# A gated-linear-attention layer on one core: TensorE's order of a head fixed from end to end, and the state updates of a PSUM bank issued together

## The chip, the cores and the metric

The kernel runs on one core of a Trainium2 chip. A core has TensorE (PE; its weight loads are listed apart as PEld), VectorE (DVE), ScalarE (ACT), GpSimd (POOL) and SyncE (SP), which issues most of the transfers. The metric is the device time of one execution in microseconds, lower is better. Before the change it is 3444.64 us, the median of three runs (3440.78 to 3449.58).

## The reference

Two layers work on 1024 latent tokens and 256 context tokens of width 1024, all in fp32. Layer 0 (neighbourhood attention and an mLSTM) is not touched. Layer 1 has 16 heads of HGRN2, a gated linear attention in both directions, which begins with a state that the context tokens leave. Cut to one head and one direction:

```python
q, f_fwd, f_bwd, i, z = split(h @ w_in)            # 128 columns each per head
f = lb + (1 - lb) * sigmoid(f_pre)                 # forget gate, per token and key column
k, lf, v = 1 - f, log(f), i
S = sum over context of (k * decay to the end) v^T # first state
# over chunks of the latent tokens, b = cumsum(lf) inside a chunk
o = (q * exp(b)) @ S + tril(q k^T with exp(b_t - b_s)) @ v
S = exp(b_last) * S + (k * exp(b_last - b))^T @ v
out = out + (rms(o_forward + o_backward) * h_norm * silu(z)) @ w_out
```

## The kernel before, in words

The loop over the 16 heads takes the span from about 2187 to 3337 us, and one head some 69 us. Products of projections are made of three TensorE products each (a high and a low part of either operand, L131 to L133).

A head h goes through these steps. `hg_f` makes its two forget gates F for 1280 tokens: 24 products 128x256 for the context and twice 24 products 128x512 for the latent tokens, each followed by a sigmoid on ACT (L983) and a scaling on DVE (L984); the forward gate comes from DRAM. `hg_vt` makes the context values (24 products, two transposes). `hg_intra` makes K = 1 - F (L1228), the sums ks (L1235) and Q (L1237) on DVE, and on PE the diagonal blocks as 16 strips of 64x64 (L1261, masked at L1248). Seven calls of `hg_level` then double the reach: each copies keys on ACT (gksel, L1297), makes 16 strips on PE (L1261) and updates Q and K on DVE (L1292). `hg_vz` makes values and the gate z of the latent tokens in eight runs of 24 products 128x256, read by ACT (L1188, L1190) and DVE (L1191). `hg_ctx` makes the two first states from the context (ACT gknc L1212, PE L1217). `hg_close` transposes the decayed keys of 8 chunks of 128 tokens (16 transposes, L1273) and ACT copies them (gkn, L1275).

`hg_scan` makes the states and the output. A backward update is a PE product (L1337) and a DVE step (L1339), seven in a chain; then each of 8 chunks has three products into the one accumulator bank `acc` (A times v L1349, Q times the backward state L1350, Q times the forward state L1351), and a forward update (L1354, DVE L1356). After 4 chunks ACT squares the bank (L1365), and DVE makes y4, the bank times z, into tile gA (L1369), which frees the bank for the other 4 chunks; POOL scales y4. `hg_out` transposes the result (L1408), ACT writes gyt (L1411), and POOL sends it to DRAM. Then POOL handles sums of output weights (`wo_sums`) and, for some heads, differences of earlier outputs (`y_diff`): two loads, a subtraction, three writes of 256 KB.

PSUM has 8 banks in the loop: two for products (mm), two for transposes (tr), three for strips and states (s), one for the accumulator (acc).

The order on each engine is set by a list scheduler, which runs a model of the engines while the program is built; code order gives the priority, `urgent()` raises it, and `issue_after(ins)` lets an instruction come only after another. Before, the eight runs of `hg_vz` are tied to the levels' strips, the gates of the next head to the last level, and everything else goes where the scheduler sees room.

Of the kernel before, what the change touches and what calls it, by code (L numbers as in the profile page):

```python
# [19 lines left out]
P = 128  # L20
# [25 lines left out]
class Prog:  # L46
# [99 lines left out]
    def proj_tr(self, ps, w, c0, t0, n):  # L146
        hh, hl = self.hh, self.hl
        s, c = slice(t0, t0 + n), slice(c0, c0 + P)
        self.dense(
# [820 lines left out]
    def hg_f(self, h, pool, w=None, run=None):  # L970
# [7 lines left out]
        for t0, n in ((LAT, CTX), (512, 512), (0, 512)):  # L978
            ps = self.ps("mm", [P, n])
            with self.tc.issue_after(run.ins) if run else ExitStack():  # L980
                self.proj_tr(ps, w, 0, t0, n)
# [3 lines left out]
        return F, Fc  # L985

    def hg_proj(self, h, pool, FF=None, run=None):
        dma = self.nc.sync.dma_start
        F, Fc = FF or self.hg_f(h, pool, run=run)
# [6 lines left out]
        return dict(F=F, Fc=Fc, q=q)  # L996
# [164 lines left out]
    def hg_vt(self, h, st, pool, w=None):  # L1161
# [5 lines left out]
        self.proj_tr(ps, w, 0, LAT, CTX)  # L1167
# [9 lines left out]
    def hg_vz(self, st, pool, runs):  # L1177
        nc, v, w = self.nc, st["v"], st["wz"]
        st["ss"] = [self.t(pool, [P, 4], F32, "gss", 2) for _ in range(2)]
        z = self.t(pool, [P, NT - 2, P], F32, "gz", 1)  # L1180
        runs = iter(runs)
        for tt in (6, 4, 2, 0):

            ps = self.ps("mm", [P, 2, 256])
            for j in range(2):
                with self.tc.issue_after(next(runs).ins):
                    self.proj_nat(ps[:, j, :], w, tt + j, 0, 256)
            nc.scalar.copy(v[:, tt : tt + 2, :], ps[:, :, 0:P])  # L1188
            sg = self.t(pool, [P, 2, P], F32, "gsg", 1)
            nc.scalar.activation(sg, ps[:, :, P:256], AF.Sigmoid)  # L1190
            nc.vector.tensor_tensor(out=z[:, tt : tt + 2, :], in0=sg, in1=ps[:, :, P:256], op=ALU.mult)  # L1191
        st["z"] = z


    def hg_ctx(self, st, pool):
# [17 lines left out]
        S = []  # L1213
        for d in range(2):
            u = self.ps("s", [P, P])
            for j in range(2):
                nc.tensor.matmul(u, lhsT=kn[:, 2 * d + j, :], rhs=v[:, 8 + j, :], start=(j == 0), stop=(j == 1))  # L1217
            s = self.t(pool, [P, P], F32, f"gS{d}", 10 if d else 2)
            nc.vector.tensor_copy(s, u)
# [4 lines left out]
    def hg_intra(self, h, st, pool):  # L1224
# [8 lines left out]
        for hf in (1, 0):  # L1233
            s = slice(hf * 512, (hf + 1) * 512)
            nc.vector.tensor_tensor(out=ks[hf], in0=K[:, 0, s], in1=K[:, 1, s], op=ALU.add)  # L1235
            for d in range(2):
                nc.vector.tensor_tensor(out=Q[:, 1 - d, s], in0=q[hf], in1=F[:, d, s], op=ALU.mult)  # L1237
        hv = dict(Q=Q, K=K, T=F, D=self.t(pool, [P, 8, 64], F32, "gD", 1))
        hv["A"] = self.t(pool, [P, 8, P], F32, "gA", 1)
# [814 lines left out]
```

## Time and profile before

| | before |
|---|---|
| median of three runs | 3444.64 us (3440.78 to 3449.58) |
| profiled execution | 3439.37 us, span 3437.3 us |
| mean granted TensorE clock | 0.994 of full speed |
| busy, share of the span | PE 97%, PEld 86%, DVE 63%, ACT 42%, POOL 24% |

The span is the part of the execution that the trace covers, and the difference of 2 us lies around it. A busy share is the time in which an engine has at least one instruction running; PE's matmuls are pipelined, so that two rows can overlap. Times in the rows of a timeline are us from the span's start, then the duration, then what the engine waited for just before, if it did.

### The profile page before, as it was taken

How to read it: one execution, taken by the hardware profiler on the slowest of the kernel's cores; microseconds unless marked ns; L12 is line 12 of the kernel's file. 1: busy time of each engine (PE TensorE's matmuls, PEld its weight loads, DVE VectorE, ACT ScalarE, POOL GpSimd, SP SyncE). 2: the span in 40 equal slices, each digit the busy share in tenths (PEclk: the TensorE clock that was granted, in tenths of full speed). 3: DMA queues.
4: the chain of work that ended last, by engine and by line, in shares of the span. 5: the costliest groups of instructions: out<-in, count | busy, mean ns of one | idle time of the engine just before them, and what ended most of it. 6: DMA issues, size and time to landing. Idle time of an engine off the chain costs nothing.

```text
span 3437.3 us, 64829 instructions
## 1 busy us (share of the span) xinstructions
PE 3329.7 (97%) x24814; PEld 2940.7 (86%) x24814; DVE 2179.7 (63%) x4965; ACT 1451.0 (42%) x3389; POOL 838.5 (24%) x1215
## 2 busy tenths in 40 slices
PE   7999999999999999999998999999999999999999
PEld 6699899998899888898877888888888888888887
DVE  5346666666645576686677555666666676667657
ACT  5335554445533444454453333333333333333343
POOL 2222222222221121221025333122232233234110
PEclk9999999999999999999999999999999999999999
DMA  7612322223234343354642333322232233224267
GB/s 250 229 53 78 92 82 73 79 67 92 82 100 138 106 143 110 121 171 142 221 132 77 105 102 101 104 70 76 87 97 88 76 96 83 76 76 101 54 187 205
DMA packets 338101, 379.80 MB, mean 110 GB/s; under 512 B 34600, under 2 KB 269800, under 8 KB 336768
## 3 DMA queue, kind: packets, MB, share of 16 engines
q1 hardware_dynamic: 286032, 236.73, 23.4%
q0 software_dynamic: 51760, 138.94, 12.9%
q8 instruction: 195, 3.19, 0.4%
q14 instruction: 114, 0.93, 0.1%
HBM read 272.31 MB, written 103.08 MB: 109 GB/s over the span
## 4 chain that ended last, share of the span: by engine, by line
PE 85%; DVE 4%; issue 4%; DMA 3%; ACT 2%; POOL 1%; SPq 1%; DVEq 0%; POOLq 0%; ACTq 0%
PE mm L131 16%; PE mm L132 15%; PE mm L133 15%; PE s L1261 4%; PE mm L923 3%; PE mm L924 3%; PE mm L925 3%; PE acc L861 2%; PE tr L841 2%; PE acc L633 2%; PE s L642 2%; PE x L133 1%; PE x L131 1%; PE x L132 1%; PE acc L1350 1%
## 5 line engine op out<-in xcount | busy, mean ns | idle before, releaser
L131 PE MATMUL mm<-wh,hh 128*128 128x256 f32 (+1 forms) x1504 | 466.2, 310 | 2.2 <-DVE graw L1550 0.8
L132 PE MATMUL mm<-wl,hh 128*128 128x256 f32 (+1 forms) x1504 | 464.1, 309 | 0.0
L133 PE MATMUL mm<-wh,hl 128*128 128x256 f32 (+1 forms) x1504 | 461.6, 307 | 0.0
L131 PE MATMUL mm<-hh,wh 128*128 128x512 f32 (+1 forms) x1160 | 421.7, 364 | 4.7 <-DVE og L959 3.1
L132 PE MATMUL mm<-hl,wh 128*128 128x512 f32 (+1 forms) x1160 | 422.9, 365 | 0.0
L133 PE MATMUL mm<-hh,wl 128*128 128x512 f32 (+1 forms) x1160 | 422.3, 364 | 0.4 <-DVE wl L74 0.4
L131 PEld LDWEIGHTS mm<-wh,hh 128*128 128x128 f32 x1504 | 284.8, 189 | 21.4 <-ACT ev L352 3.4
L132 PEld LDWEIGHTS mm<-wl,hh 128*128 128x128 f32 x1504 | 284.9, 189 | 12.3 <-issue 0.7
L133 PEld LDWEIGHTS mm<-wh,hl 128*128 128x128 f32 x1504 | 284.7, 189 | 12.0 <-issue 0.5
L131 PE MATMUL mm<-wzh,hh 128*128 128x256 f32 x960 | 284.8, 297 | 0.0
L133 PE MATMUL mm<-wzh,hl 128*128 128x256 f32 x960 | 272.6, 284 | 0.0
L132 PE MATMUL mm<-wzl,hh 128*128 128x256 f32 x960 | 272.4, 284 | 0.0
L131 PEld LDWEIGHTS mm<-hh,wh 128*128 128x128 f32 x1160 | 219.3, 189 | 41.7 <-ACT ev L371 4.2
L133 PEld LDWEIGHTS mm<-hh,wl 128*128 128x128 f32 x1160 | 219.2, 189 | 33.1 <-DVE wl L74 1.0
L132 PEld LDWEIGHTS mm<-hl,wh 128*128 128x128 f32 x1160 | 219.5, 189 | 29.7 <-issue 0.2
L131 PEld LDWEIGHTS mm<-wzh,hh 128*128 128x128 f32 x960 | 183.3, 191 | 7.2
L1297 ACT COPY gksel<-gK 128x1024 f32<-128x1024 f32 x96 | 110.5, 1151 | 178.6 <-DVE gK L1292 77.3
L132 PEld LDWEIGHTS mm<-wzl,hh 128*128 128x128 f32 x960 | 184.2, 192 | 0.0
L133 PEld LDWEIGHTS mm<-wzh,hl 128*128 128x128 f32 x960 | 183.5, 191 | 0.0
L74 DVE TENSOR_TENSOR wl<-wraw,wh 128x512 fp32r<-128x512 f32 x176 | 120.1, 690 | 74.9 <-ACT wh L73 71.7
L1292 DVE TENSOR_TENSOR gQ<-gQ,gF 128x1024 f32<-128x1024 f32 x112 | 142.3, 1271 | 34.6 <-PE s L1261 34.5
L1292 DVE TENSOR_TENSOR gK<-gK,gF 128x1024 f32<-128x1024 f32 x112 | 152.3, 1360 | 6.7
(562 smaller groups left out, 8512.3 us busy)
## 6 DMA issues: line engine op xcount, KB each, us to landing
wraw<-in_wab_dram SPq DMA_DIRECT2D x108, 256.0 KB
wraw<-yd SPq DMA_DIRECT2D x92, 256.0 KB
br<-in_wc_dram SPq DMA_DIRECT2D x64, 256.0 KB
md<-ev POOLq DMA_DIRECT2D x60, 256.0 KB, 2.6
wraw<-in_wc_dram SPq DMA_DIRECT2D x120, 128.0 KB
mloz<-md SPq DMA_DIRECT2D x40, 256.0 KB
s<-gyt POOLq DMA_DIRECT2D x36, 256.0 KB, 5.3
adar<-in_wada_dram SPq DMA_DIRECT2D x16, 512.0 KB
```

Source lines behind the costliest of these rows:

```text
L74: nc.vector.tensor_tensor(out=lo, in0=x, in1=hi.bitcast(F32), op=ALU.subtract)
L131: mm(ps, lhsT=lh(k), rhs=rh(k), start=(start and k == 0), stop=False, skip_group_check=skip)
L132: mm(ps, lhsT=lh(k), rhs=rl(k), start=False, stop=False, skip_group_check=skip)
L133: m = mm(ps, lhsT=ll(k), rhs=rh(k), start=False, stop=(stop and k == nk - 1), skip_group_check=skip)
L633: nc.tensor.matmul(num, lhsT=qc[:, j, :], rhs=C[d][:, j, :], start=False, stop=(j == 1))
L642: nc.tensor.matmul(u, lhsT=st["k"][c][:, j * P : (j + 1) * P], rhs=vw, start=True, stop=True)
L923: mm(ps, lhsT=yh[k], rhs=w.h(kk), start=(kk == 0), stop=False)
L924: mm(ps, lhsT=yh[k], rhs=w.l(kk), start=False, stop=False)
L925: mm(ps, lhsT=yl[k], rhs=w.h(kk), start=False, stop=(kk == 8 * len(qs) - 1))
L1261: return self.nc.tensor.matmul(out[s], lhsT=lhsT, rhs=rhs, start=True, stop=True, tile_position=(0, b * 64))
L1292: nc.vector.tensor_tensor(out=v, in0=v, in1=tot, op=ALU.mult)
L1297: m = nc.scalar.copy(ksel.rearrange("p (b s i) -> p b s i", s=2, i=h), pick(K))
```

## The change

The order of a head on PE is now written out. `last_pe` holds PE's last instruction of the piece before, and `seg()` lets a piece be issued only after it. The whole row of a head is: the diagonal strips; the strips of level 0 directly behind them; transposes of the context values; run 0 of `hg_vz`; level 1; first half of the previous head's `hg_out`; run 1; level 2; its second half; run 2; `hg_ctx`; then a level and a run in turn to level 6 and runs 6 and 7; `hg_close` for chunks 4 to 7; the next head's gate products for the context; `hg_close` for chunks 0 to 3; the backward updates of chunks 4 to 7, then 1 to 3, and the forward ones of chunks 0 to 3; 24 gate products 128x512; the forward updates of chunks 4 to 6; 24 gate products 128x512; the scan of chunks 0 to 3 and of chunks 4 to 7; and the next head's 24 products for the context values.

All updates of a bank are issued together (`hg_states`), and DVE's chain of steps reads them afterwards (`hg_chain`). So all states of both directions are kept: gS0 and gS1 have 8 buffers each (2 and 10 before). Besides, the sigmoid is written into z itself, the tile gA is taken only at level 6, `hg_out`, `wo_sums` and `y_diff` of a head come at levels 1 and 2 of the next, K's sums and Q are urgent, and `hg_ctx` uses one bank for both directions. 

```diff
+    @contextmanager
+    def seg(self):
+        with self.tc.issue_after(self.last_pe.ins) if self.last_pe else ExitStack():
+            yield
...
+        def part(t0, n):
             ps = self.ps("mm", [P, n])
-            with self.tc.issue_after(run.ins) if run else ExitStack():
-                self.proj_tr(ps, w, 0, t0, n)
+            with self.seg():
+                m = self.proj_tr(ps, w, 0, t0, n)
+            if self.pinned:
+                self.last_pe = m
...
+        parts = [lambda x=x: part(*x) for x in ((LAT, CTX), (512, 512), (0, 512))]
+        return F, Fc, parts
...
-                with self.tc.issue_after(next(runs).ins):
-                    self.proj_nat(ps[:, j, :], w, tt + j, 0, 256)
+                with self.seg():
+                    self.last_pe = self.proj_nat(ps[:, j, :], w, tt + j, 0, 256)
+                if j == 0:
+                    yield
+            z2 = z[:, tt : tt + 2, :]
             nc.scalar.copy(v[:, tt : tt + 2, :], ps[:, :, 0:P])
-            sg = self.t(pool, [P, 2, P], F32, "gsg", 1)
-            nc.scalar.activation(sg, ps[:, :, P:256], AF.Sigmoid)
-            nc.vector.tensor_tensor(out=z[:, tt : tt + 2, :], in0=sg, in1=ps[:, :, P:256], op=ALU.mult)
-        st["z"] = z
...
+        u = self.ps("s", [P, 2, P])
         for d in range(2):
-            u = self.ps("s", [P, P])
             for j in range(2):
-                nc.tensor.matmul(u, lhsT=kn[:, 2 * d + j, :], rhs=v[:, 8 + j, :], start=(j == 0), stop=(j == 1))
-            s = self.t(pool, [P, P], F32, f"gS{d}", 10 if d else 2)
-            nc.vector.tensor_copy(s, u)
+                nc.tensor.matmul(u[:, d, :], lhsT=kn[:, 2 * d + j, :], rhs=v[:, 8 + j, :], start=(j == 0), stop=(j == 1))
+        for d in range(2):
+            s = self.t(pool, [P, P], F32, f"gS{d}", 8)
+            nc.vector.tensor_copy(s, u[:, d, :])
...
+        halves = [(hf, slice(hf * 512, (hf + 1) * 512)) for hf in (1, 0)]
+        with self.urgent():
+            for hf, s in halves:
+                nc.vector.tensor_tensor(out=ks[hf], in0=K[:, 0, s], in1=K[:, 1, s], op=ALU.add)
+            for hf, s in halves:
+                for d in range(2):
+                    nc.vector.tensor_tensor(out=Q[:, 1 - d, s], in0=q[hf], in1=F[:, d, s], op=ALU.mult)
...
-        with self.urgent():
+        with self.urgent(), self.seg():
...
-        runs = [m]
+        self.last_pe = m
+        tiles = self.hg_vz(st, pool)
         for lev in range(7):
-            runs.append(self.hg_level(hv, lev, pool))
+            if lev == 6:
+                hv["A"] = self.t(pool, [P, 8, P], F32, "gA", 1)
+            self.hg_level(hv, lev, pool)
+            if lev in (1, 2) and prev:
+                prev(lev)
+            next(tiles)
             if lev == 2:
                 S = self.hg_ctx(st, pool)
-        return hv, S, runs
+                if prev:
+                    prev(3)
+        next(tiles)
+        return hv, S
...
+    def hg_states(self, st, H, d, c0, c1):
+        v = st["v"]
+        u = self.ps("s", [P, 4, P])
+        with self.seg():
+            for c in range(c0, c1):
+                m = self.nc.tensor.matmul(
+                    u[:, c - c0, :], lhsT=H["kn"][c // 4][d][:, c % 4, :], rhs=v[:, c, :], start=True, stop=True
+                )
+        self.last_pe = m
+        return {c: u[:, c - c0, :] for c in range(c0, c1)}
+
+
+    def hg_chain(self, H, d, S, u, order, pool):
+        for c in order:
+            s = self.t(pool, [P, P], F32, f"gS{d}", 8)
+            self.nc.vector.scalar_tensor_tensor(
+                out=s, in0=S[c], scalar=H["T"][:, d, c : c + 1], in1=u[c], op0=ALU.mult, op1=ALU.add
+            )
+            S[c + 1 if d == 0 else c - 1] = s
...
-        sb = {7: Sb}
-        for c in range(7, 0, -1):
-            if c in (7, 3):
-                u4 = self.ps("s", [P, 4, P])
-            u = u4[:, c % 4, :]
-            nc.tensor.matmul(u, lhsT=H["kn"][c // 4][1][:, c % 4, :], rhs=v[:, c, :], start=True, stop=True)
-            s = self.t(pool, [P, P], F32, "gS1", 10)
-            nc.vector.scalar_tensor_tensor(
-                out=s, in0=sb[c], scalar=H["T"][:, 1, c : c + 1], in1=u, op0=ALU.mult, op1=ALU.add
-            )
-            sb[c - 1] = s
         for c in range(8):
             cs = slice(c * P, (c + 1) * P)
             if c % 4 == 0:
                 o4 = self.ps("acc", [P, 4, P])
-                u4 = self.ps("s", [P, 4, P])
             o = o4[:, c % 4, :]
-            nc.tensor.matmul(o, lhsT=H["A"][:, c, :], rhs=v[:, c, :], start=True, stop=False)
-            nc.tensor.matmul(o, lhsT=H["Q"][:, 0, cs], rhs=sb[c], start=False, stop=False)
-            nc.tensor.matmul(o, lhsT=H["Q"][:, 1, cs], rhs=Sf, start=False, stop=True)
-            if c < 7:
-                u = u4[:, c % 4, :]
-                nc.tensor.matmul(u, lhsT=H["kn"][c // 4][0][:, c % 4, :], rhs=v[:, c, :], start=True, stop=True)
-                s = self.t(pool, [P, P], F32, "gS0", 2)
-                nc.vector.scalar_tensor_tensor(
-                    out=s, in0=Sf, scalar=H["T"][:, 0, c : c + 1], in1=u, op0=ALU.mult, op1=ALU.add
-                )
-                Sf = s
...
                 for h in range(16):
-                    self.hg_vt(h, st, pool, None if h else wv)
-                    hv, S, runs = self.hg_intra(h, st, pool)
-                    self.hg_vz(st, pool, runs)
-                    self.hg_close(hv, pool)
-                    self.hg_scan(st, hv, S, pool)
-                    if h < 15:
-                        st = self.hg_proj(h + 1, pool, run=runs[7])
+                    hv, (Sf, Sb) = self.hg_intra(h, st, pool, prev)
+                    nxt, parts = self.hg_proj(h + 1, pool) if h < 15 else (None, [lambda: None] * 3)
+                    self.hg_close(hv, 1, pool)
+                    parts[0]()
+                    self.hg_close(hv, 0, pool)
+                    Sf, Sb = {0: Sf}, {7: Sb}
+                    ub = self.hg_states(st, hv, 1, 4, 8)
+                    ub.update(self.hg_states(st, hv, 1, 1, 4))
+                    uf = self.hg_states(st, hv, 0, 0, 4)
+                    self.hg_chain(hv, 1, Sb, ub, range(7, 0, -1), pool)
+                    self.hg_chain(hv, 0, Sf, uf, range(4), pool)
+                    parts[1]()
+                    uf = self.hg_states(st, hv, 0, 4, 7)
+                    self.hg_chain(hv, 0, Sf, uf, range(4, 7), pool)
+                    parts[2]()
+                    self.hg_scan(st, hv, Sf, Sb, pool)
+                    st = nxt
                     if h == 15:
                         rh.close()
                         yp = es.enter_context(tc.tile_pool(name="oy", bufs=1, side="right"))
                         last = [self.t(yp, [P, 512], F32R, t, 1) for t in ("lasth", "lastl")] + [yp]
-                    y15 = self.hg_out(h, hv["A"], pool, self.yd2, last)
-                    if h < 14:
-                        self.wo_sums(h // 2, h % 2, pool, ("gknc", 1), ("gEc", 1))
-                    if h in (11, 12):
-                        self.wo_sums(7, h - 11, pool, ("gyt", 1), ("wraw", 3))
-                    if 0 < h < 9:
-                        self.y_diff(h - 1, pool)
+
+                    def prev(lev, h=h, A=hv["A"]):
+                        if lev == 3:
+                            return sums(h)
+                        self.hg_out(h, A, pool, self.yd2, None, (0,) if lev == 1 else (4,))
+
+                    def sums(h):
+                        if h < 14:
+                            self.wo_sums(h // 2, h % 2, pool, ("gknc", 1), ("gEc", 1))
+                        if h in (11, 12):
+                            self.wo_sums(7, h - 11, pool, ("gyt", 1), ("wraw", 3))
+                        if 0 < h < 9:
+                            self.y_diff(h - 1, pool)
+
+                    if h == 15:
+                        y15 = self.hg_out(h, hv["A"], pool, self.yd2, last)
+                    if h < 15:
+                        self.hg_vt(h + 1, st, pool)
```

Three places show how the order moved. The line numbers of the changed kernel are larger by 9 to 24 in these functions. **PE around the two halves of the scan**, a head of the middle; before (acc_27565 is the first half's bank, acc_27600 the second half's):

```order
L131 MATMUL mm_28047<-wzh_27773,hh_20307 128x256
L1351 MATMUL acc_27565<-gS_5478_27577,gQ_24854 128x128 [waits DVE_49]
L1354 MATMUL s_27566<-gv_27049,gkn_27533 128x128
L1349 MATMUL acc_27565<-gv_27049,gA_27092 128x128
L1350 MATMUL acc_27565<-gS_5470_27553,gQ_24854 128x128
...
L133 MATMUL mm_28047<-wzh_27773,hl_20308 128x256
L1351 MATMUL acc_27565<-gS_5479_27583,gQ_24854 128x128 [waits DVE_49]
L1354 MATMUL s_27566<-gv_27049,gkn_27533 128x128
L1354 MATMUL s_27601<-gv_27049,gkn_27519 128x128 [waits DVE_49]
L1349 MATMUL acc_27600<-gv_27049,gA_27092 128x128 [waits DVE_49]
L1350 MATMUL acc_27600<-gS_5469_27550,gQ_24854 128x128
```

and with the change (acc_27669 and acc_27691):

```order
L1383 MATMUL acc_27669<-gS_5468_27599,gQ_24854 128x128
L1381 MATMUL acc_27669<-gv_26995,gA_27416 128x128
L1382 MATMUL acc_27669<-gS_5463_27589,gQ_24854 128x128
L1383 MATMUL acc_27669<-gS_5469_27601,gQ_24854 128x128
L1381 MATMUL acc_27691<-gv_26995,gA_27416 128x128 [waits DVE_49]
L1382 MATMUL acc_27691<-gS_5462_27587,gQ_24854 128x128
...
L1382 MATMUL acc_27691<-gS_5422_27244,gQ_24854 128x128
L1383 MATMUL acc_27691<-gS_5475_27640,gQ_24854 128x128
L131 MATMUL mm_27736<-hh_20307,wzh_27714 128x256
L132 MATMUL mm_27736<-hl_20308,wzh_27714 128x256
L133 MATMUL mm_27736<-hh_20307,wzl_27713 128x256
L131 MATMUL mm_27736<-hh_20307,wzh_27714 128x256
```

Before, gate, value and z products stood between the scan's products; now both halves stand in one row, and the products of the next head (the last four rows) come behind them.

**DVE at the same place.** Before, and then with the change:

```order
L1356 SCALAR_TENSOR_TENSOR gS_5478_27577<-gS_5477_27571,gT_27293,s_27566 128x128 [waits PE_49]
L1248 TENSOR_TENSOR gD_27836<-s_27838,glm_4216_20266 128x512 [waits PE_49]
L1356 SCALAR_TENSOR_TENSOR gS_5479_27583<-gS_5478_27577,gT_27293,s_27566 128x128 [waits DVE_49,PE_49]
L1237 TENSOR_TENSOR gQ_24854<-gq_27731,gF_27632 128x512 [waits DMAHW4_49,PE_49]
L1237 TENSOR_TENSOR gQ_24854<-gq_27731,gF_27632 128x512 [waits PE_49]
L1356 SCALAR_TENSOR_TENSOR gS_5480_27589<-gS_5479_27583,gT_27293,s_27566 128x128 [waits DVE_49,PE_49]
L1205 TENSOR_SCALAR gq_27926<-gFc_27633 128x512 [waits DVE_49]
L1356 SCALAR_TENSOR_TENSOR gS_5484_27606<-gS_5480_27589,gT_27293,s_27601 128x128 [waits DVE_49]
L1369 TENSOR_TENSOR gA_27092<-acc_27565,gz_27301 128x512 [waits Activation_49,Pool_49]
```

```order
L993 TENSOR_SCALAR gF_27494<-gF_27494,lb_114 128x512 [waits Activation_49]
L1242 TENSOR_SCALAR gK_27767<-gF_27494 128x2048 [waits DVE_49]
L1253 TENSOR_TENSOR gQ_24854<-gq_27512,gF_27494 128x512 [waits DMAHW4_49,PE_49]
L1250 TENSOR_TENSOR gkn_27770<-gK_27767 128x512 [waits DVE_49]
L1250 TENSOR_TENSOR gkn_27769<-gK_27767 128x512
L1253 TENSOR_TENSOR gQ_24854<-gq_27512,gF_27494 128x512 [waits PE_49]
L1315 TENSOR_TENSOR gK_27767<-gK_27767,gF_27494 128x2x512 [waits DVE_49,Activation_49]
L1393 TENSOR_TENSOR gA_27416<-acc_27669,gz_27081 128x512 [waits Activation_49,Pool_49]
L1253 TENSOR_TENSOR gQ_24854<-gq_27510,gF_27494 128x512 [waits DMAHW2_49,PE_49]
L1253 TENSOR_TENSOR gQ_24854<-gq_27510,gF_27494 128x512 [waits PE_49]
L1393 TENSOR_TENSOR gA_27416<-acc_27691,gz_27081 128x512 [waits Activation_49]
```

y4 (L1369, now L1393, from the first bank) stood among the forward steps (L1356, now L1366) and the next head's diagonal; now it stands behind the next head's whole gate, K, ks, Q of one half and the first update of K, and the steps are done earlier.

**ACT and PE at the close of a head.** ACT before, and then with the change (wzh and wh are casts of the next weights, gkn the copies of transposed keys):

```order
L1275 COPY gkn_26029<-tr_26024 128x512 [waits PE_49]
L1275 COPY gkn_26036<-tr_26031 128x512 [waits PE_49]
L983 ACTIVATE gFc_26143<-mm_26156 128x256 [waits PE_49]
L73 CAST wzh_26283<-wraw_26299 128x512 [waits DMAHW3_49,DMAHW2_49]
L73 CAST wh_26890<-wraw_26891 128x512 [waits DMAHW4_49]
L73 CAST wh_26896<-wraw_26897 128x512 [waits DMAHW5_49]
L1275 COPY gkn_26043<-tr_26038 128x512 [waits PE_49]
L1275 COPY gkn_26050<-tr_26045 128x512 [waits PE_49]
L983 ACTIVATE gF_26142<-mm_26183 128x512 [waits PE_49]
```

```order
L1298 COPY gkn_26039<-tr_26034 128x512 [waits PE_49]
L1298 COPY gkn_26046<-tr_26041 128x512 [waits PE_49]
L992 ACTIVATE gFc_26015<-mm_26048 128x256 [waits PE_49]
L1298 COPY gkn_26080<-tr_26075 128x512 [waits PE_49]
L73 CAST wzh_26234<-wraw_26250 128x512 [waits DMAHW3_49,DMAHW2_49]
L1298 COPY gkn_26087<-tr_26082 128x512 [waits PE_49]
L73 CAST wh_26757<-wraw_26758 128x512 [waits DMAHW4_49]
L73 CAST wh_26763<-wraw_26764 128x512 [waits DMAHW5_49]
L992 ACTIVATE gF_26014<-mm_26125 128x512 [waits PE_49]
```

PE with the change (tr are the transposes, s the banks of the updates):

```order
L1296 MATMUL tr_26075<-ident_82,gK_25555 128x128 x3
L1296 MATMUL tr_26082<-ident_82,gK_25555 128x128 [waits Activation_49]
L1296 MATMUL tr_26082<-ident_82,gK_25555 128x128 x3
L1356 MATMUL s_26089<-gv_25523,gkn_26046 128x128 x4
L1356 MATMUL s_26094<-gv_25523,gkn_26087 128x128 [waits Activation_49]
L1356 MATMUL s_26094<-gv_25523,gkn_26087 128x128 x2
L1356 MATMUL s_26098<-gv_25523,gkn_26080 128x128 x4
L131 MATMUL mm_26125<-hh_20307,wh_26017 128x512 [waits DVE_49]
```

The last gkn copy now stands behind the fourth wzh cast as both copies of its half did before, but the two copies are split around it, and PE's second group of updates reads it directly, ahead of the gate products.

91 lines of the change are left out of this document (49 added, 42 removed).

## The prediction, made before the changed kernel was run

> **What bounds the kernel now.** I read the page first, then the busy time by head, then what TensorE's two queues waited for in the layer-1 loop, then single rows of the timeline. The page's first part and two rows and the sum of the windows by head (us, then busy us and instructions of PE, PEld, DVE, ACT, POOL, the granted clock, DMA share, GB/s):
>
> ```profile
> PE 3329.7 (97%) x24814; PEld 2940.7 (86%) x24814; DVE 2179.7 (63%) x4965; ACT 1451.0 (42%) x3389; POOL 838.5 (24%) x1215
> ...
> 2573.40:2641.80 68.40, 64.87 (x660) 59.81 (x659) 45.90 (x73) 24.11 (x54) 19.96 (x29) 1.00 0.28 88
> 2779.30:2849.70 70.40, 66.44 (x661) 61.29 (x660) 45.79 (x73) 23.94 (x53) 21.15 (x27) 0.98 0.35 90
> ...
> sum 1041.20, PE 983.53 PEld 906.41 DVE 684.44 ACT 360.63 POOL 288.97; mean PE 65.57 PEld 60.43 DVE 45.63 ACT 24.04 POOL 19.26
> ```
>
> TensorE bounds everything; DVE is at 66% in the loop. One head takes 1041.20 / 15 = 69.4 us, of which PE is idle 3.8. So the change, which leaves the instructions as they are, can win a few us per head, and can lose as many as it puts in TensorE's way. Its waits in the loop, from the queue that loads weights:
>
> ```profile
> PEld s L1354 <- DVE gS L1356: 23.0, 15, 1.6
> PEld s L1337 <- DVE gS L1339: 18.5, 31, 0.6
> PEld acc L1350 <- DVE gS L1339: 9.5, 15, 0.6
> PEld s L1354 <- DVE gS L1339: 8.8, 14, 0.6
> PEld s L1217 <- ACT gknc L1212: 8.4, 15, 0.6
> PEld acc L1349 <- DVE gA L1369: 8.0, 15, 0.9
> PEld s L1261 <- DVE gQ L1237: 4.7, 15, 0.3
> ```
>
> The first four are the state updates, where PE and DVE take turns in one PSUM bank. The timeline shows one turn:
>
> ```profile
> 2593.09 0.49 PE L1337 MATMUL s<-gv,gkn 128*128 128x128 f32 x2 [0.37 <-DVE gS L1339]
> 2594.02 0.49 PE L1337 MATMUL s<-gv,gkn 128*128 128x128 f32 x2 [0.44 <-DVE gS L1339]
> ...
> 2595.27 0.39 PE L1351 MATMUL acc<-gS,gQ 128*128 128x128 f32 x2
> ...
> 2596.39 0.39 PE L1350 MATMUL acc<-gS,gQ 128*128 128x128 f32 x2
> ```
>
> A turn costs 2594.02 - 2593.09 = 0.93 us, while five steps of products that wait for nothing take 1.12, or 0.224 each: 0.7 us lost per turn.
>
> **What it removes.** All updates of a bank are issued before DVE reads it, so the first four waits go: 23.0 + 18.5 + 9.5 + 8.8 = 59.8 us. DVE's fourteen chain steps remain, but under F's products. The wait for gA (8.0) changes its form and is priced anew below; gQ's 4.7 goes too, since 24 products stand ahead of the diagonal strips and cover DVE. In all -72.5 us. The diagonal strips and level 0 now stand together, which saves one change from 256-wide products to strips and back per head. Around such a group:
>
> ```profile
> 2562.97 0.28 PE L133 MATMUL mm<-wzh,hl 128*128 128x256 f32 x1
> 2563.18 1.15 PE L1261 MATMUL s<-gQ,gksel 128*64 128x64 f32 x32
> 2564.26 0.39 PE L131 MATMUL mm<-wzh,hh 128*128 128x256 f32 x1
> 2564.48 0.28 PE L132 MATMUL mm<-wzl,hh 128*128 128x256 f32 x1
> ```
>
> From product to product it is 1.51 us; with 0.24 for two products at 0.12 and 1.15 for the strips (the last one's tail in it), at least 0.12, at most 0.34 is the change: 16 x 0.25 = -4 us. The context matmuls share one bank instead of two and may wait on the copy gknc a little longer, since the previous head's output now stands ahead of it on ACT: from the 8.4 us of now, between 0 and +10; I take +5.
>
> **What it adds, first: the second half of the scan.** One accumulator bank serves both halves, and chunk 4 waits until DVE's y4 has read chunks 0 to 3. Before, other products stood between; now nothing does: the next head's 24 context products come after the whole scan. And y4 stands on DVE behind the next head's F, K, Q, sums and the first update of K. All of these start only once F's last product, the instruction ahead of the scan, is done. Their durations, in the same head:
>
> ```profile
> 2588.30 0.60 ACT L983 ACTIVATE gF<-mm 128x512 f32<-128x512 f32 x1 [4.11 <-PE mm L133]
> ...
> 2588.93 0.55 DVE L984 TENSOR_SCALAR gF<-gF,lb 128x512 f32<-128x512 f32 x1 [3.50 <-ACT gF L983]
> ...
> 2589.65 1.22 DVE L1228 TENSOR_SCALAR gK<-gF 128x2048 f32<-128x2048 f32 x1
> ...
> 2594.81 0.68 DVE L1235 TENSOR_TENSOR gkn<-gK 128x512 f32<-128x512 f32 x1
> 2595.60 1.23 DVE L1292 TENSOR_TENSOR gK<-gK,gF 128x1024 f32<-128x1024 f32 x1
> ...
> 2598.98 0.69 DVE L1237 TENSOR_TENSOR gQ<-gq,gF 128x512 f32<-128x512 f32 x1
> ...
> 2603.38 0.69 DVE L1369 TENSOR_TENSOR gA<-acc,gz 128x512 f32<-128x512 f32 x1
> ```
>
> 0.60 + 0.55 + 1.22 + 2 x 0.69 + 2 x 0.68 + 1.23 + 0.69 = 7.0 us from the last product. The first half of the scan is 12 products of 0.224, 2.7 us. PE then stands 7.0 - 2.7 = 4.3 us; successive DVE rows overlap by some 0.1, so I take 4.2. Fifteen heads have a next head: +63 us. The bounds: 0.5 (the 8.0 us of now, by head) if DVE were early, and 5 if each handover costs 0.1.
>
> **What it adds, second: a copy behind a weight load.** On ACT the last copy of a head's transposed keys (gkn) now stands behind the cast of the fourth piece of the next weights, which waits for its DMA. Before, both key copies stood behind it too, and PE ran F's 512-wide products meanwhile; now PE's second bank of state updates waits for that copy and F's products stand behind it. The rows of ACT and PE at this place, a head with a late piece and one with an early piece, and ACT's total:
>
> ```profile
> 2571.26 0.28 PE L133 MATMUL mm<-wzh,hl 128*128 128x256 f32 x1
> ...
> 2573.42 1.04 PE L1273 MATMUL tr<-ident,gK 128*128 128x128 f32 x8
> ...
> 2580.54 0.62 ACT L73 CAST wzh<-wraw 128x512 fp32r<-128x512 f32 x1 [4.61 <-DMA wraw<-in_wc_dram]
> ...
> 2582.62 1.06 ACT L1275 COPY gkn<-tr 128x512 f32<-128x512 f32 x2
> ...
> 2847.82 0.37 ACT L1188 COPY gv<-mm 128x256 f32<-128x256 f32 x1 [1.89 <-PE mm L133]
> ...
> 2852.67 0.62 ACT L73 CAST wzh<-wraw 128x512 fp32r<-128x512 f32 x1 [0.51 <-DMA wraw<-in_wc_dram]
> ...
> ACT wzh L73 <- DMA wraw<-in_wc_dram: 56.8, 20, 5.5
> ```
>
> In the changed order PE runs, after the last z product, 8 transposes (about 0.9 us, from 1.04 less the tail), 24 products of 0.12 (2.9), 8 transposes (0.9) and 4 updates (0.9): 5.6 us. The copy is done 2580.54 + 0.62 + 0.53 - 2571.4 = 10.3 us after that product: a stall of 4.7 us. With the early piece the same sum is 2852.67 + 1.15 - 2847.8 - 5.6 = 0.4. The late pieces are those of heads 1 to 8, in which POOL sends out 256 KB pieces of differences that take this long:
>
> ```profile
> s<-gyt POOLq DMA_DIRECT2D x36, 256.0 KB, 5.3
> ...
> s<-gknc POOLq DMA_DIRECT2D x16, 256.0 KB, 4.3
> ```
>
> The change sends these at level 2 of the next head instead of behind the head's output; counted on POOL's queue, they still come out near the end of the z products, so I keep the collision. The bounds are 0.4 x 15 = 6 us with no collision and 4.7 x 15 = 70 with it everywhere; In both heads the stall is about the wait that ACT shows (4.7 for 4.61, 0.4 for 0.51), so ACT's whole row, 56.8 us in 20 waits, bounds it a second way; some of the 20 belong to earlier pieces, which PE needs later. I take two thirds: +38 us, as 3.6 in 8 heads and 1.3 in 7.
>
> Without the clock: -72.5 - 4 + 5 + 63 + 38 = +30 us.
>
> **The clock.** The granted clock falls to half for one window of 3.41 us when the window before it was idle enough. Two pairs of rows show where that starts:
>
> ```profile
> 2453.03:2456.44 3.41, 2.03 (x11) 1.46 (x12) 2.23 (x6) 0.59 (x2) 0.00 (x0) 1.00 0.00 0
> 2456.44:2459.85 3.41, 3.41 (x34) 3.19 (x34) 1.49 (x2) 0.00 (x0) 0.00 (x0) 0.50 0.02 5
> ...
> 2729.51:2732.92 3.41, 2.16 (x13) 1.59 (x14) 2.14 (x6) 0.29 (x2) 0.00 (x0) 1.00 0.00 0
> 2732.92:2736.34 3.42, 3.42 (x54) 3.23 (x52) 2.19 (x4) 0.00 (x0) 0.00 (x0) 1.00 0.02 5
> ```
>
> PE busy 2.03 us of a window was followed by 0.50, 2.16 was not. A stall of 4.2 us always leaves some window with 2.1 us of idle or more, so with at most 1.3 busy: each of the 15 scans should be followed by half-clock windows, and so should most of the 3.6 us stalls. The price is the difference of the two heads above, 70.40 - 68.40 = 2.0, or 1.8 where part of the slow window is itself a wait. Five heads of the 15 have one now (those at 0.98). With 15 + 6 - 5 = 16 more: +29 us. The Trainium skill, "TensorE: Matmul & The Clock Gate", section "HAM oscillation — how this bites in real kernels", puts it as no idle gaps of TensorE beyond some 3.4 us; read as one wholly idle window, a gap of 4.2 us would seldom do it, and the sum would end at +30, which is rival A. The rows above, in which 2.03 us of work did not keep the clock, speak against that reading.
>
> **Sum.** 3439.4 (the profiled execution; span 3437.3) + 30 + 29 = 3498. The median of the runs shown, 3444.64, is 5 above the profiled one, so I write 3500.
>
> **Rivals.** (A) The clock holds: a window must be nearly empty. The five drops of now remain, the time is 3439 + 30 + 5 = 3474. For it: 3.6 us stalls split over two windows; against it: the rows of the clock. (B) Faster: the weight piece is early everywhere (6 instead of 38), because the differences leave before its loads, and y4's wait is 2.5 us, because DVE runs the queue ahead of y4 in less than the single rows say (+38 instead of 63). Then -72.5 - 4 + 5 + 38 + 6 = -28, no window is idle enough, and the time is 3444 - 28 = 3416. It decides from a wait at the second half below about 3 us together with casts within 3 us of their issue. Against it: DVE's order names eight instructions, all with rows. (C) Worse: the piece is late in all heads (70) and each stall leaves two slow windows or one each (30 - 5 at 2.0 = 50): -72.5 - 4 + 10 + 63 + 70 + 50 = +116; with half of the excess over the forecast, 3528. For it: POOL's longer list at levels 1 and 2 shifts the writes onto the piece. (D) The change does nothing: DVE's chain and the copies still find other products on PE to hide under, 3440 to 3450. The order of instructions speaks against it, for PE has one fixed row per head.
>
> **Chances.** Forecast 0.52, A 0.16, B 0.12, C 0.14, D 0.06. A change within 0.3% (about 10 us, 3434 to 3455) can't be told from none here. Slower: the forecast, C, and nearly all of A, 0.80; the same: D and the edges of A and B, 0.10; faster: 0.10. The range runs from 3445 (A with a cheaper weight piece) to 3540 (C), and the forecast's own part of it is 3480 to 3520.
>
> **What would show it.** Right: among TensorE's waits, the second half's first product of `acc` for DVE's y4 at about 4 us a head, the second bank of state updates for ACT's gkn at 1 to 5 us, no waits for gS; granted clock 0.96 to 0.97 in the loop's heads, half-clock windows just after the scans. Wrong: y4's wait under 2 us, casts that wait less than 1 us, or waits that are there with the clock at 1.00. If DVE's rows ahead of y4 are not those eight, the first term falls.

## The result and the profile after

The changed kernel takes 3483.64 us (median of four runs, 3481.01 to 3490.05), the kernel before 3444.13 on the same chip: ratio 1.0116, 95% interval 1.0097 to 1.0135. It is slower by 39.5 us, where 56 had been forecast.

The busy time of the loop, from the first head's close to the last one's, of the changed kernel (us, then busy us and instructions of PE, PEld, DVE, ACT, POOL, clock, DMA share, GB/s), and what PE's weight queue waited for in it (us in total, times, longest):

```profile
2227.10:3303.30 1076.20, 990.41 (x9873) 929.62 (x9872) 678.60 (x1081) 365.48 (x780) 284.83 (x396) 0.95 0.28 80
```

```profile
PEld acc L1381 <- DVE gA L1393: 64.0, 15, 4.3
PEld s L1356 <- ACT gkn L1298: 17.2, 14, 3.0
PEld s L1230 <- ACT gknc L1225: 13.7, 15, 0.9
```

The 15 heads take 1076 us; before they took 1041. The waits of the state updates are gone from the list. The wait for y4 stands at the top with 4.3 us a head, and the mean clock of the loop is 0.95 in place of 0.99. One such stall on PE, and the five clock windows around it:

```profile
2533.32 0.39 PE L1383 MATMUL acc<-gS,gQ 128*128 128x128 f32 x2
2537.80 0.79 PE L1381 MATMUL acc<-gv,gA 128*128 128x128 f32 x2 [4.10 <-DVE gA L1393]
2538.39 0.64 PE L1382 MATMUL acc<-gS,gQ 128*128 128x128 f32 x2
2538.82 0.63 PE L1383 MATMUL acc<-gS,gQ 128*128 128x128 f32 x2
...
2542.66 0.63 PE L1383 MATMUL acc<-gS,gQ 128*128 128x128 f32 x2
```

```profile
2530.13:2533.55 3.42, 3.42 (x28) 3.23 (x27) 1.81 (x3) 0.60 (x1) 0.00 (x0) 1.00 0.00 0
2533.55:2536.96 3.41, 0.15 (x2) 0.00 (x0) 3.41 (x5) 2.89 (x9) 0.29 (x1) 1.00 0.00 0
2536.96:2540.37 3.41, 2.57 (x12) 2.57 (x13) 0.79 (x2) 0.00 (x0) 2.31 (x3) 0.50 0.00 0
2540.37:2543.79 3.42, 3.42 (x18) 3.42 (x18) 0.89 (x2) 0.37 (x3) 0.00 (x0) 0.50 0.00 0
2543.79:2547.20 3.41, 3.41 (x50) 3.28 (x51) 1.21 (x3) 1.48 (x7) 1.99 (x3) 1.00 0.00 0
```

The window with the stall in it is followed by two windows at half clock, in which a product of the scan takes (2542.66 - 2538.82) / 9 = 0.43 us in place of 0.224. The stall is paid a second time. Counted over the loop, 29 windows run at half clock, before it was 5.

What DVE and ACT do in that stall:

```profile
2532.27 1.23 DVE L1242 TENSOR_SCALAR gK<-gF 128x2048 f32<-128x2048 f32 x1
2533.52 0.69 DVE L1253 TENSOR_TENSOR gQ<-gq,gF 128x512 f32<-128x512 f32 x1
2534.13 1.29 DVE L1250 TENSOR_TENSOR gkn<-gK 128x512 f32<-128x512 f32 x2
2535.33 0.68 DVE L1253 TENSOR_TENSOR gQ<-gq,gF 128x512 f32<-128x512 f32 x1
2535.93 1.22 DVE L1315 TENSOR_TENSOR gK<-gK,gF 128x1024 f32<-128x1024 f32 x1
2537.07 0.68 DVE L1393 TENSOR_TENSOR gA<-acc,gz 128x512 f32<-128x512 f32 x1
```

```profile
2533.59 1.52 ACT L1320 COPY gksel<-gK 128x1024 f32<-128x1024 f32 x1 [1.93 <-DVE gK L1242]
2535.02 0.27 ACT L1390 ACTIVATE gjk<-acc 128x128 f32<-128x128 f32 x1
...
2536.38 0.20 ACT L1390 ACTIVATION_READ_ACCUMULATOR gjk<-acc 128x1 f32 x1
```

DVE goes through the row that was forecast and is not idle from the next head's gate to y4. The ACT rows show something the forecast had left out: the four squares, which read the same bank, stand behind the next head's first gksel copy and end at 2536.58, only 0.5 us before y4 starts. The bank is held by two chains of nearly the same length.

### The profile page after: what moved, and what is told of

Read it like the earlier page. It is cut to its first block, busy times and chain, and to the rows that moved or that the text cites. A ratio compares the mean times of both kernels' runs of the same rounds, so it can differ in the third digit from the quotient of the medians.

```text
span 3480.7 us, 64774 instructions
## 1 busy us (share of the span) xinstructions
PE 3340.1 (96%) x24814; PEld 2962.8 (85%) x24814; DVE 2171.1 (62%) x4965; ACT 1457.0 (42%) x3389; POOL 826.7 (24%) x1215
## 4 chain that ended last, share of the span: by engine, by line
PE 84%; DVE 5%; DMA 4%; issue 3%; ACT 2%; SPq 1%; POOL 0%; ACTq 0%; DVEq 0%; POOLq 0%
PE mm L131 15%; PE mm L132 15%; PE mm L133 15%; PE s L1285 4%; PE acc L861 2%; PE mm L923 2%; PE mm L924 2%; PE mm L925 2%; PE tr L841 2%; PE x L131 2%; PE x L133 2%; PE x L132 2%; PE acc L633 2%; PE s L642 2%; PE acc L1381 1%
## 5 line engine op out<-in xcount | busy, mean ns | idle before, releaser
L1315 DVE TENSOR_TENSOR gK<-gK,gF 128x1024 f32<-128x1024 f32 x112 | 144.1, 1287 | 6.9 <-ACT gksel L1320 0.5
```

The source lines that it names most:

```text
L1315: nc.vector.tensor_tensor(out=v, in0=v, in1=tot, op=ALU.mult)
```

## The experiments

Each kernel below is an edit of the changed kernel, if nothing else is said. Times are medians beside the kernel before on the same chip (3443.5 to 3444.7). The change itself was timed only in the runs above, so a difference to the change is one to its median, 3483.64. Half-clock windows are counted in the loop, each of 3.41 us.

### y4 ahead on DVE

```diff
-            nc.vector.tensor_tensor(out=y4, in0=o4, ...)
+            y = nc.vector.tensor_tensor(out=y4, in0=o4, ...)
+            self.y4 = self.y4 if c == 7 else y
...
-        with self.urgent():                    # ks and Q of the next head
+        with self.urgent(), self.tc.issue_after(self.y4.ins) if h else ExitStack():
```

> The changed kernel with one thing moved: on DVE, y4 of the first half stands directly behind the next head's K (L1242), ahead of its sums and Q. Theory: PE's wait at the second half of the scan is DVE's order, 4.3 us a head, and it costs a second time through the clock. Then the wait falls from 64 us to 0.7-1.0 us a head (11 to 15 us), the half-clock windows of the loop fall from 29 to about 5, and the time is 3484 - 50 - 30 = about 3404. Rival: the half-clock windows come from somewhere else in the fixed row (the short products, the wait for gkn); then they stay near 29 and the time is 3484 - 50 = about 3434.

Measured: 3467.02 us, ratio 1.0069 (1.0053 to 1.0085). The wait hardly moved:

```profile
PEld acc L1381 <- DVE gA L1393: 58.2, 15, 3.9
...
2530.97 0.19 ACT L1390 ACTIVATION_READ_ACCUMULATOR gjk<-acc 128x1 f32 x1
...
2531.26 0.69 DVE L1393 TENSOR_TENSOR gA<-acc,gz 128x512 f32<-128x512 f32 x1 [3.15 <-ACT gjk L1390]
```

y4 now stands right behind K on DVE, and DVE waits 3.15 us for ACT's squares: both expectations missed the second chain. "Waits for DVE" in PE's list had named the last of two. Only 5.8 us of wait are gone, yet the time fell by 16.6: 16 windows run at half clock in place of 29.

### The squares ahead on ACT, alone and with y4

```diff
-                nc.scalar.activation(jk, o4[:, i, :], AF.Square, ...)
+                q = nc.scalar.activation(jk, o4[:, i, :], AF.Square, ...)
+                self.sq = q if c == 3 else self.sq
...
+                with self.tc.issue_after(self.sq.ins) if hasattr(self, "sq") and lev == 0 else ExitStack():
                     m = nc.scalar.copy(ksel..., pick(K))
```

> The changed kernel with one thing moved on ACT: the four squares of the first half stand ahead of the next head's first gksel copy, y4 stays where it is on DVE. Theory after the first runs: the bank waits for two chains of nearly equal length, DVE's (K, sums, Q, K's update, then y4, 7.0 us) and ACT's (gksel 1.5 us, four squares of 0.4, then y4), so that either moved alone moves little. Then the wait at the second half stays at 60 to 64 us and the time within 8 us of 3484. Rival: ACT's chain is the one that decides and DVE's is not; then the wait falls to about 2.5 us a head, 38, and the time to about 3450.

Measured: 3454.06 us, ratio 1.0031 (1.0019 to 1.0043); wait 47.7 us, 3.2 a head; 16 half-clock windows. Between the two expectations: with gksel later, the scheduler put K's update behind y4, so that DVE's chain lost its 1.2 us too. This run therefore shortens both chains, and does not show ACT's alone.

> The changed kernel with both moved: y4 behind K on DVE, and the squares of the first half ahead of gksel on ACT. Two-chain theory: the bank is free after four squares (1.7 us) and y4 (0.7), so the wait is about 2.6 us a head, 39 us, 25 us less, and with less idle per window the half-clock windows fall as well, below 16, worth 10 to 20 us: 3440 to 3450. Rival (a third chain is as long): the wait stays above 55 and the time above 3460.

Measured: 3434.06 us, ratio 0.9974 (0.9965 to 0.9983), below the time that was expected; the wait is what was expected:

```profile
PEld acc L1382 <- DVE gA L1395: 39.3, 15, 2.6
```

64.0 in the change, 58.2 with DVE's chain shortened, 47.7 with ACT's and K's update off DVE's, 39.3 with all of both: the two chains stand side by side, and the rest, 2.6 us, is the squares (1.6) and y4 (0.7) themselves, one after the other, with the handovers. The half-clock windows fell to 13.

### The stall filled with work that nobody needs

```diff
+            if c == 3:
+                x = self.ps("mm", [P, 256])
+                with self.seg():
+                    for k in range(32):
+                        m = nc.tensor.matmul(x, lhsT=self.hh[:, k % 8, 0:P], rhs=self.hh[:, k % 8, 0:256], start=True, stop=True)
+                self.last_pe = m
```

> The changed kernel with 32 products 128x256 more per head, written to a product bank that nobody reads, between the two halves of the scan (3.84 us of work at 0.12, in a stall of 4.3 us). Nothing is taken off DVE's way, so the second half starts when it did. Theory (the idle time itself halves the clock afterwards): half-clock windows fall from 29 to about 5, and the time falls by what they cost, about 30 us, to 3454, with 512 products more. Rival (the clock falls for another reason): 3484 or a little more.

Measured: 3459.73 us, ratio 1.0046 (1.0032 to 1.0059). The wait row has 6.6 us left, 4 windows of the loop run at half clock, and the kernel is 24 us faster than the change although PE does 3.8 us a head more and the second half starts no earlier. So it is the idle time that halves the clock. The loop's row, as above:

```profile
2228.00:3276.30 1048.30, 1013.02 (x10352) 952.11 (x10351) 681.67 (x1081) 365.20 (x780) 282.98 (x396) 0.99 0.29 82
```

Without the added products (15 x 32 x 0.12 = 57.6) PE is busy for 955.4 us in place of 990.4: 35 us less with 25 half-clock windows fewer, or 1.4 us a window. The time fell by less, because the gkn wait grew from 17.2 to 23.0 us and 6 us were lost outside the loop.

### The gkn copy ahead of the weight cast

```diff
+            with self.tc.issue_after(self.kcopy.ins) if (tag, i) == ("wz", 3) else ExitStack():
                 self.split(his[i]..., los[i]..., raw...)
```

> The changed kernel with the last gkn copy ahead of the fourth wzh cast on ACT, so that PE's second group of updates no longer waits behind a weight load. By the plain sum the 17.2 us of that wait go down to 0.3 us a head, and the time is 3484 - 12 to 17 = 3467 to 3472. By the lock theory (15 of the 16 heads take 71.0 to 71.8 us, and 21 clock windows of 3.413 are 71.7: a head that does less begins its stall earlier in a window and gets more half-clock time instead) the time stays within 4 us of 3484, except what heads 7, 8 and 10 lose, which are out of the lock.

Measured: 3459.13 us, ratio 1.0043 (1.003 to 1.0055): 24.5 us less than the change, more than the wait itself, which went from 17.2 to 2.9. The strict lock theory falls here (and in the change 12 of 15 heads had the length that it names, not 15 of 16). Half-clock windows fell from 29 to 21, and the first 11 heads now alternate, three of them here:

```profile
2439.60:2509.10 69.50, 64.72 (x660) 60.88 (x659) 45.43 (x72) 24.32 (x52) 19.17 (x27) 0.98 0.27 86
2509.10:2579.60 70.50, 65.72 (x660) 61.88 (x659) 45.25 (x72) 24.24 (x52) 19.39 (x29) 0.95 0.27 86
2579.60:2649.00 69.40, 64.62 (x660) 60.78 (x659) 44.93 (x72) 24.34 (x52) 17.53 (x25) 0.98 0.27 86
```

69.5 + 70.5 = 140.0 us is 41 windows of 3.413 (139.9), where 3.413 is the mean of the 82 windows from 2453.03 to 2732.92 in the rows of before: two heads go with the windows, where it had been one head with 21 (71.7).

### More work per head

```diff
             with self.seg():
+                for k in range(4 if self.pinned and t0 == 0 else 0):
+                    self.nc.tensor.matmul(ps, lhsT=self.hh[:, k, 0:P], rhs=self.hh[:, k, 0:512], start=True, stop=True)
                 m = self.proj_tr(ps, w, 0, t0, n)
```

> The changed kernel with 4 products 128x512 more per head ahead of the last 24 gate products (0.91 us at 0.227), written to a bank that is then overwritten. By the plain sum +13.6 us, 3497. By the lock theory the head stays at 21 windows and the half-clock time shrinks by what is added: 3484 within 4 us, with a higher mean clock.

Measured: 3487.17 us (3483.09 to 3497.1), ratio 1.013 (1.0111 to 1.0149), so +3.5 us on the medians, and the intervals of the ratios overlap. In the two profiled executions the loop is 3.2 us longer (1079.4 against 1076.2) with the same idle time (85.7 and 85.8), and the half-clock windows fell from 29 to 22. So of 13.6 us of added work some 10 are taken back by the clock: a head that gets longer meets the windows in another place. Together with the run above, a weak form stands: around this period small differences of work do not pass one to one into time, in either direction.

### One part alone: the batched updates on the kernel before

```diff
+        chain(1, sb, states(1, 4, 8), range(7, 3, -1))
+        chain(1, sb, states(1, 1, 4), range(3, 0, -1))
+        chain(0, sf, states(0, 0, 4), range(4))
+        chain(0, sf, states(0, 4, 7), range(4, 7))
```

`states` issues the products of a bank, `chain` the DVE steps behind them, ahead of the loop over chunks; gS0 and gS1 have 8 buffers, the sigmoid goes into z.

> The kernel before with one part of the change: all state updates of a bank are issued before DVE reads it (8 states kept of either direction, the sigmoid written into z so that they fit). The order of TensorE stays the scheduler's. Theory (the first term of the sum, 59.8 us of turns between PE and DVE, was real idle time): 3444 - 45 to 60 = 3384 to 3400. Rival: the turns had overlapped with waits that come anyway (y4, the first level), so that most of it comes back as other waits: 3430 to 3444.

Measured: 3353.54 us, ratio 0.9743 (0.973 to 0.9756): 90 us faster than the kernel before and 130 faster than the change.

```profile
2228.20:3181.40 953.20, 948.82 (x9883) 890.86 (x9881) 691.85 (x1082) 361.44 (x782) 285.88 (x384) 1.00 0.32 90
```

```profile
PEld s L1217 <- ACT gknc L1212: 4.7, 7, 1.0
...
PEld s L1261 <- DVE gQ L1237: 2.5, 7, 0.4
```

PE is idle for 4.4 us in the whole loop, and no window is at half clock. That is the fastest kernel of this study.

### Level 0 with the diagonal strips, on top of that

```diff
+        runs[0] = runs[1]
         return hv, S, runs
```

> The batch on the kernel before, and besides level 0 ahead of the first run of z products, so that its strips can stand directly behind the diagonal strips, as the change has them. By the sum: one change from products to strips less per head, 16 x 0.25 = -4 us, 3350. Rival: the first run of z products covered level 0's K, Q and gksel; without it the strips of level 0 wait 1 to 2 us a head: 3368 to 3385.

Measured: 3356.34 us (3353.25 to 3357.78), the same ratio 0.9743 (0.973 to 0.9757). Neither the 4 us gain nor the loss is there. But the order that the run was to give did not come about: in 14 of the 16 heads the scan's second half and four transposes of the output, 28 products, stand between the two groups of strips. One such head, and then the change, where they do stand together:

```profile
2630.95 1.15 PE L1262 MATMUL s<-gq,gkn 128*64 128x64 f32 x32
...
2636.11 1.54 PE L1262 MATMUL s<-gQ,gksel 128*64 128x64 f32 x32
```

```profile
2617.93 1.15 PE L1285 MATMUL s<-gq,gkn 128*64 128x64 f32 x32
2618.91 1.52 PE L1285 MATMUL s<-gQ,gksel 128*64 128x64 f32 x32
```

So this run does not test the term. The wait for gQ is 5.1 us in place of 2.5, one for y4 of 6.6 us appeared, and the one for gknc (4.7) went.

### The fixed row loosened

```diff
-            with self.seg():
+            with ExitStack():          # the scan's products
...
-        with self.seg():
-            self.last_pe = self.proj_tr(ps, w, 0, LAT, CTX)
+        self.proj_tr(ps, w, 0, LAT, CTX)
...
-        self.last_pe = m
```

> The changed kernel with the scan's products and the next head's 24 context products taken out of the fixed row (the scheduler places them), all else as it is. Theory: what costs is that nothing may stand between the halves; free products go there, the wait for gA falls from 64 us to under 20, the half-clock windows below 12, and the time to 3400 to 3430. Rival: what the scheduler may place there (24 products, 2.9 us) is not taken or does not reach over the 4.3 us; then 3450 or more.

Measured: 3440.18 us, ratio 0.9988 (0.9979 to 0.9997). The wait for gA is gone, but

```profile
PEld s L1284 <- DVE gQ L1252: 35.5, 15, 2.4
PEld s L1355 <- ACT gkn L1297: 23.6, 14, 5.4
```

the products and diagonal strips that now fill the gap had covered Q's second half behind the scan: level 0 waits 2.4 us a head, and 18 windows are at half clock. The wait row met the expectation, the windows and the time did not; the rival's 3450 was not reached either.

```diff
     def seg(self):
-        with self.tc.issue_after(self.last_pe.ins) if self.last_pe else ExitStack():
-            yield
+        yield
```

> The changed kernel without any fixed order on TensorE: the same code order, no piece tied to the one before. Batched updates, later output, urgent K and Q, and the shared context bank stay. Theory (the batch is worth 90 us as in the run on the kernel before, and the fixed row is what costs): near the batch alone, 3345 to 3375. Rival (the other parts cost too, the late output or the urgent K and Q): 3400 or more.

Measured: 3395.78 us, ratio 0.9858 (0.9844 to 0.9871). Without pins the change is 88 us faster, but 42 behind the batch alone, just short of the rival's 3400. What is left of the change costs too: the largest wait in PE's own queue is

```profile
PE s L1284 <- DVE gQ L1314: 30.3, 15, 2.3
```

Q's update before a strip group, and 8 windows are at half clock. The weight queue puts the same stop down to ACT's gate z (33.1 us), so which engine ends it is open, and which of the remaining parts brings it was not taken apart.

### All stalls of the fixed row mended

The edits of y4, squares and gkn together, and the next head's context products moved between the halves of the scan:

```diff
+            if c == 4 and mid:
+                self.last_pe = m
+                mid()                  # hg_vt of the next head
```

> The changed kernel with both moved, the last gkn copy ahead of the fourth weight cast, and the next head's 24 context products (2.9 us) between the halves of the scan in place of behind them. Theory: the wait at the second half goes to under 0.5 us a head, the wait for gkn to under 5 us in all, the half-clock windows to about 5: 3484 - 60 - 14 - 30 = 3380. Rival: what stood behind the scan had covered Q and the first gksel copy, so level 0 now waits 1 to 2 us a head: 3395 to 3410.

Measured: 3394.12 us, ratio 0.986 (0.9846 to 0.9873), between the two expectations and 1 us from the rival's 3395. No window of the loop is at half clock, and no wait for gA is left; the strips now wait instead, as the rival had it for level 0 (PE's own queue):

```profile
PE s L1286 <- DVE gQ L1316: 18.5, 30, 0.7
PE s L1231 <- ACT gknc L1226: 10.1, 15, 0.7
PE s L1286 <- DVE gQ L1254: 7.3, 16, 1.1
```

A head takes 65.9 us, against 63.5 with the batch and a free order.

## Why the prediction was right, and where not

**The balance.** From the batch alone to the change it is 3483.6 - 3353.5 = 130 us. In the loop PE is idle 1076.2 - 990.4 = 85.8 us in place of 4.4, which is 81 more; it is busy 990.4 in place of 948.8, which is 42 more for the same products, and 29 half-clock windows at 1.4 us are 41; the remaining 7 lie outside the loop. So the change is a gain of 90 us and a loss of 130. Of the loss, 88 go when the fixed row is loosened everywhere (3483.6 to 3395.8), and 42 remain with the other parts, which were not separated.

**The removed waits** (-72.5). That they were real idle time is shown by the batch alone, whose gain was even larger: 88 us in the loop (1041.2 - 953.2). Beyond the 59.8 us of turns the other waits of the list fell too (y4's 8.0 to nothing, the context copy's 8.4 to 4.7, gQ's 4.7 to 2.5), and with them the five half-clock windows, some 7 us at 1.4. Those the forecast had taken off in its clock term (15 + 6 - 5), so that its first term was short by 88 - 7 - 72.5 = 8.5 us.

**Diagonal and level 0** (-4): not tested, since the run that was meant for it kept the two groups apart. The rows agree with it: in the batch alone the two groups with one product on either side take 1.51 (2567.86 to 2569.37) and 1.91 us (2638.70 to 2640.61), or 2.94 without the four products of 0.12; in the change they take 3.04 together (2617.72 to 2620.76), or 2.80 without two products, and that holds two transposes of up to 0.19. So an estimate from these rows is 0.14 to 0.33 us a head less, 2 to 5 us.

**The context copy** (+5): 13.7 - 8.4 = 5.3 us. Right in size; what the copy stands behind was not looked at.

**The second half of the scan** (+63): 64.0 us, 4.3 a head. The size and DVE's row were right. The cause was incomplete: ACT's squares behind gksel were a second chain half a microsecond shorter. That this chain, which the forecast did not look at, was not the longer one is luck, and the price that the rivals gave for an earlier y4 (2.5 us a head) could not have come from DVE alone. That y4 waits for the squares at all, although both only read, is seen in the row at 2531.26. The Trainium skill, "PSUM — Partial Sum Buffer", section "PSUM bank collisions raise a hardware error", has it that two engines must not touch the same 32 partitions of one bank at once, two readers included, and that the compiler back end's scheduler adds a dependency for it; this case's trace agrees as far as it goes, with y4 starting 0.1 us after the last square.

**The copy behind the weight cast** (+38): the wrong size, 17.2 us. The step that failed is "they still come out near the end of the z products, so I keep the collision". The writes do come out there, 0.9 us ahead of the last z product (2510.97), but the collision does not follow. POOL's three writes of a difference now start earlier against the weights:

```profile
2511.97 1.66 ACT L73 CAST wzh<-wraw 128x512 fp32r<-128x512 f32 x3
2516.41 0.62 ACT L73 CAST wzh<-wraw 128x512 fp32r<-128x512 f32 x1 [0.36 <-DMA wraw<-in_wc_dram]
...
2510.11 0.57 POOL L1425 DMA_DIRECT2D sy<-gknc  x1 [0.30 <-POOL gknc L1423]
2510.68 1.08 POOL L1425 DMA_DIRECT2D s<-gknc  x2
```

They start 1.9 us before the first cast (2511.97). In the kernel before they started 1.8 us behind it, in the head that the forecast went by, and were on their way together with the fourth piece:

```profile
2572.27 1.67 ACT L73 CAST wzh<-wraw 128x512 fp32r<-128x512 f32 x3
...
2574.08 0.56 POOL L1400 DMA_DIRECT2D sy<-gknc  x1 [0.30 <-POOL gknc L1398]
```

The fourth cast waits 0.36 us in the change's head, where it had waited 4.61. The heads of both traces line up: writes that start 0.6 to 1.9 us behind the first cast go with waits of 2.8 to 4.6 us (all eight heads of before), 0.8 behind with 2.3, 0.1 ahead with 1.6, and 0.9 to 1.9 ahead with at most 0.4, once 1.0. So the writes are very likely the reason, but no run moved them alone; in heads 7 to 9 the wait is still 1 to 2.3 us.

**The clock** (+29): about 34 us, 24 windows more at the 1.4 us of the filled stall. The mechanism was right, and that the total came so near is luck: 29 half-clock windows where 21 were forecast, at 1.4 us in place of 1.8. The prediction took one window per stall; two follow. The window in which the stall ends runs at half clock, busy for 2.57 us, and so does the one behind it. The Trainium skill, "TensorE: Matmul & The Clock Gate", section "HAM oscillation — how this bites in real kernels", tells of gaps beyond 3.4 us; read as one wholly idle window, a gap of 4.3 us would cost a window only where it holds a whole one. Here 12 of 15 heads have a mean clock of 0.95 and one of 0.93, two or three half-clock windows each, and in the rows of before a window with 2.03 us of work was followed by half clock. Rival A, which rests on that reading, fell. Rival B was right about the early weight piece and C about two slow windows for a stall; neither held as a whole.

**Outside the loop** the change lost 8.4 us that no term held: the loop begins 2 us later, and what follows it takes 177.4 us (3480.7 - 3303.3) in place of 171.0 (3437.3 - 3266.3), where PE waits 4.3 us in one piece for a cast of outputs that are read back (0.7 before), and two windows run at half clock (none before).

With these sizes it is -72.5 - 4 + 5 + 64 + 17 + 34 + 8.4 = +52, against 43 between the two profiled executions (3482.66 - 3439.37); the 9 left over are about the 8.5 that the first term was short of. The forecast, +59 in this sum, was some 15 us too high: the weight cast was priced 21 too high and the first term gained 8.5 more than it said, against 5 more at the clock, 1 at the scan and 8.4 outside the loop. So part of the closeness comes from errors of opposite sign.

## What to carry to other kernels

Batch what lets two engines take turns, and leave the order free: the same idea was worth 90 us alone and -40 with an order that took away what could stand in the gaps. Before an order is fixed, look for each single-buffered bank at every chain that frees it, on all engines that read it, and for what covers each; moving cover from one gap opens the next. On a kernel that TensorE bounds, a stall of a few microseconds is paid again in part through the clock, here some 34 us on 81 of waits (64.0 and 17.2).

## What the hardware showed that was not expected

A period may tie itself to the clock's windows. With the change, 12 of the 15 heads take 71.0 to 71.9 us, close to the 71.7 of 21 windows of 3.413; with the gkn copy moved, two heads together take 41 in the first 11 heads. The reason would be that a stall that begins earlier in a window brings more half-clock time. This is argued from the rows; the two runs on it agree in part only (work of 13.6 us added cost 3.5, while 14.3 us of waits removed gave 24.5).

The price of a half-clock window is steadier. By PE's busy time in the loop and the count of windows, each against the change, it is 1.4 us with the stall filled (35.0 over 25 windows) and with y4 ahead on DVE (990.4 - 972.7 = 17.7 over 13), and 1.3 with both chains shortened (990.4 - 969.3 = 21.1 over 16).
